# A two-layer decoder trunk on one core: ScalarE's reads of VectorE results issued a step later, the gated output in five stages, and eight weight residuals moved from GpSimd to VectorE

## The chip, the core and the metric

The kernel runs on one core of a Trainium2 chip. TensorE multiplies, VectorE, ScalarE and GpSimd work on the elements, and SyncE's queue issues the loads and stores. Each engine takes its instructions strictly in the order in which the program wrote them for that engine, and waits on semaphores for the others. The metric is the device time of one execution in microseconds (us). For the kernel before, three runs gave 849.0, 849.64 and 850.5 us.

## What is computed

Two layers over one sequence of 256 tokens of width 2048, in float32. Layer 0 runs retention heads and latent attention heads side by side and is not touched by the change. Layer 1, the Conformer convolution module, is:

```
h = rms_norm(x, norm_g)
a, b, gate = jnp.split(h @ w_in, 3, axis=-1)
u = a * jax.nn.sigmoid(b)
u = lax.conv_general_dilated(
    u, conv_w[:, None, :].astype(u.dtype), window_strides=(1,),
    padding=[(CONV_KERNEL - 1, 0)], dimension_numbers=('NWC', 'WIO', 'NWC'),
    feature_group_count=CONV_WIDTH) + conv_b
u = jax.nn.silu(layer_norm(u, ln_g, ln_b))
return x + (u * jax.nn.silu(gate)) @ w_out
```

The convolution is depthwise, causal and 31 taps long. The layer norm needs the mean and the variance over all 2048 channels, so that nothing behind it can start before the last channel has been convolved.

## The kernel before

All activations lie transposed: 128 channels on the partitions, 256 tokens along the row. The 2048 channels are 16 blocks of 128.

**Three products for one.** Each float32 weight tile `raw` is split in two parts that TensorE can multiply at full rate: ScalarE rounds it (`whi`, L167), and the residual `raw - whi` is taken by VectorE or GpSimd (`wlo`, L88 by way of `tt`). The activations are split the same way. `mm3` (L193 to L195) then issues three matmuls: high by high, high by low, low by high.

**The stream.** `Stream` hands out the weights in units of 1 MB, each in two halves. The table at its start says for each unit whether VectorE (`V`) or GpSimd (`G`) takes the residual. `half(u, h)` is called by TensorE's loop before it uses a half: it issues the residual three halves ahead (`lo_to(j + 3)`) and the rounding four halves ahead (`hi_to(j + 4)`), and then calls `tick()`. There are three buffers for `raw`, five for `whi` and four for `wlo`.

**The clock of the program.** `clock` counts halves: a half is 24 matmuls. `later(n, fn)` writes `fn` into the program n steps from now; `tick()` writes what is due, `tick(True)` does so in the middle of a half. Nothing of this runs on the chip: it decides the order in which instructions stand in each engine's queue.

**The order of layer 1.** `pair` multiplies 256 output columns (two blocks of 128) over all 2048 inputs, in four halves. Sixteen pairs give a and b of one channel block each; `glu` takes each pair: `norm_cols` multiplies it in PSUM by the token norm `R1` (VectorE), ScalarE takes the sigmoid, VectorE multiplies (`f`), and `conv_add` queues the 31 taps of this block. Two blocks are convolved in turn, a tap is one `stt` on VectorE. `pace` writes up to 2.88 us of such taps into the program at each step, by fixed costs for each operation; `spend` books other work of VectorE against the same budget. The residuals of the weights are not booked. `shift` and `centre` subtract an estimate of the mean, `centre_sq` squares on ScalarE, `centre_add` sums up both. Behind the sixteen pairs, eight pairs give the gate (`cgt`), with `norm_cols` and a SiLU each.

**The end of the layer norm.** When the last block is summed, `norm_conv` puts the sums through two matmuls (L985, L986), works out mean and scale, and then the result z in eight parts of 512 columns: `za` subtracts, scales (VectorE) and takes the SiLU (ScalarE), `zb` multiplies by the gate (VectorE) and rounds (ScalarE), `zc` takes the residual (VectorE). A list `z_todo` holds these steps; `z_tick` writes two of them at each step. The first product of the output, `kgroup` over `u_co1` with eight PSUM columns, eats one block k (half a part of z) per half; `z_need` sees to it that the part stands in the program before its use. Four more pairs (`u_co2`) and the stores end the kernel.

Of the kernel before, what the change touches and what calls it, by code (L numbers as in the profile page):

```python
# [10 lines left out]
AF = mybir.ActivationFunctionType  # L11
ALU = mybir.AluOpType
# [4 lines left out]
T = 256  # L17
# [8 lines left out]
TAPS = 31  # L26
# [22 lines left out]
def body(ctx, tc, a):  # L49
    nc = tc.nc  # L50
    act = nc.scalar.activation
    V = nc.vector
    G = nc.gpsimd
# [27 lines left out]
    def auxps():  # L81
        return psx.tile([P, 512], F32, tag="aux", name=nm("aux"))
# [4 lines left out]
    def tt(out, in0, in1, op, eng=None):  # L87
        (eng or V).tensor_tensor(out=out, in0=in0, in1=in1, op=op)  # L88

    def stt(out, in0, s, in1, op0, op1):  # L90
        V.scalar_tensor_tensor(out=out, in0=in0, scalar=s, in1=in1, op0=op0, op1=op1)  # L91
# [10 lines left out]
    def later(n, fn):  # L102
        due.append((clock[0] + n, len(due), fn))
# [84 lines left out]
    st = Stream()  # L188

    def mm3(ps, l, r, start, stop):  # L190
        (lh, ll), (rh, rl) = l, r
        mm = nc.tensor.matmul
        mm(ps, lh, rh, start=start, stop=False, skip_group_check=True)  # L193
        mm(ps, lh, rl, start=False, stop=False, skip_group_check=True)  # L194
        mm(ps, ll, rh, start=False, stop=stop, skip_group_check=True)  # L195
# [26 lines left out]
    u_gate = [st.add(a["w_in"][20 + i], V) for i in range(16)]  # L222
    u_out = [st.add(a["w_out"][i], V) for i in range(16)]
    u_ab = [st.add(a["c_in"][i], V if i < 2 else G) for i in range(32)]
    u_cg = [st.add(a["c_in"][32 + i], G) for i in range(16)]
    u_co1 = [st.add(a["c_out1"][i], V) for i in range(8)]
    u_co2 = [st.add(a["c_out2"][i], V) for i in range(8)]

# [95 lines left out]
    def kgroup(units, ncols, nk, rhs, hook=None, bank=mmps):  # L324
        banks = [bank() for _ in range(ncols // 2)]
        total = len(units) * nk
        k = 0
        for u in units:
            for h in range(2):
                if hook:  # L330
                    hook(k)
                hi, lo = st.half(u, h)
                for i in range(nk // 2):
                    r = rhs(k)
                    cols = []
                    for c in range(ncols):
                        o = (i * ncols + c) * P
                        ps = banks[c // 2][:, (c % 2) * T:(c % 2 + 1) * T]
                        if k > 0:
                            mm3(ps, (hi[:, o:o + P], lo[:, o:o + P]), r, False, k == total - 1)  # L340
                            continue
                        for n in range(2):
                            nc.tensor.matmul(ps, hi[:, o:o + P], r[n], start=c % 2 == 0 and n == 0, stop=False, skip_group_check=True)
                        cols.append((ps, lo[:, o:o + P]))
                    for ps, wl in cols:
                        nc.tensor.matmul(ps, wl, r[0], start=False, stop=False, skip_group_check=True)
                    k += 1
        return banks

    def pair(us, rhs):  # L350
        ps = mmps()
        for k in range(KT):
            if k % 4 == 0:
                hi, lo = st.half(us[k // 8], k // 4 % 2)
            elif k % 4 == 2:
                tick(True)
            for c in range(2):
                w = slice((k % 4 * 2 + c) * P, (k % 4 * 2 + c + 1) * P)
                mm3(ps[:, c * T:(c + 1) * T], (hi[:, w], lo[:, w]), rhs(k), k == 0 and c == 0, k == KT - 1)
        return ps  # L360
# [430 lines left out]
    for j in range(8):  # L791
        o = (j % 4) * 512
        ps = pair(u_gate[2 * j:2 * j + 2], xrhs)
# [23 lines left out]
    for j in range(8):  # L817
        ps = pair(u_out[2 * j:2 * j + 2], mrhs)
        o = (j % 4) * 512
# [28 lines left out]
    def upad(c, lo, n):  # L848
        o = (c % 7) * UP + lo
        return upt[c // 7][:, o:o + n]  # L850
# [7 lines left out]
    def spend(us):  # L858
        budget[0] -= us
# [65 lines left out]
    def ds(c):  # L925
        return kk(dd, c)
# [48 lines left out]
    done4 = [False]  # L975

    zh, zl = [], []
    z_todo = []
    ln_done = [False]
    held = []  # L980
    gates = [0]

    def norm_conv():
        lps = auxps()
        nc.tensor.matmul(lps[:, 0:T], ones[:, :], sums[:, 0:T], start=True, stop=True)  # L985
        nc.tensor.matmul(lps[:, T:512], ones[:, :], sums[:, T:512], start=True, stop=True)  # L986
        mu = tmp()
        V.tensor_scalar(out=mu[:, 0:T], in0=lps[:, 0:T], scalar1=1.0 / D, scalar2=None, op0=ALU.mult)
        tt(mu[:, T:512], mu[:, 0:T], mu[:, 0:T], ALU.mult)
        stt(mu[:, T:512], mu[:, T:512], -float(D), lps[:, T:512], ALU.mult, ALU.add)  # L990
        ls = e1[:, 0:T]
        rs_chain(ls, mu[:, T:512], D)
        nc.scalar.preload_act_table_set("silu_and_others")
        zh.extend([slot(12, F32R), slot(7, F32R)])
        zl.extend([slot(9, F32R), slot(10, F32R)])

        def pr(j):
            return dd[j // 4][:, (j % 4) * 512:(j % 4 + 1) * 512]

        def za(j):  # L1000
            d = pr(j)
            tt(two(d), two(d), both(mu[:, 0:T]), ALU.subtract)
            tt(two(d), two(d), both(ls), ALU.mult)
            for k in (2 * j, 2 * j + 1):
                act(ds(k), ds(k), AF.Silu, bias=cb[:, CB["lb"] + k:CB["lb"] + k + 1],
                    scale=cb[:, CB["lg"] + k:CB["lg"] + k + 1])

        def zb(j):
            d = pr(j)
            o = (j % 4) * 512  # L1010
            tt(d, d, cgt[j // 4][:, o:o + 512], ALU.mult)
            act(zh[j // 4][:, o:o + 512], d, AF.Copy)

        def zc(j):
            o = (j % 4) * 512
            tt(zl[j // 4][:, o:o + 512], pr(j), zh[j // 4][:, o:o + 512].bitcast(F32), ALU.subtract)

        for j in range(9):
            if j < 8:
                z_todo.append((0, lambda j=j: za(j)))  # L1020
            if j > 0:
                z_todo.append((j, lambda j=j: zb(j - 1)))
                z_todo.append((0, lambda j=j: zc(j - 1)))
        ln_done[0] = True
        for f in held[0]:
            f()
        z_tick()

    def z_step():
        if z_todo and z_todo[0][0] <= gates[0]:  # L1030
            z_todo.pop(0)[1]()
            return True
        return False

    def z_tick():
        for _ in range(2):
            z_step()
        if z_todo:
            later(1, z_tick)

    def z_need(k):
        while len(z_todo) > max(0, 24 - (1 + 3 * (k // 2 + 1))) and z_step():
            pass

    def conv_fin(c):
        ps = accs[c]
# [13 lines left out]
    def norm_cols(ps):  # L1060
        tt(two(ps[:, :]), two(ps[:, :]), both(R1[:, :]), ALU.mult)
        spend(0.6)

    def glu(c, ps):
        sg = tmp()
        norm_cols(ps)
        act(sg[:, 0:T], ps[:, T:512], AF.Sigmoid)  # L1067

        def f():
            tt(upad(c, TAPS - 1, T), ps[:, 0:T], sg[:, 0:T], ALU.mult)  # L1070
            conv_add(c)

        later(1, f)

    def conv_add(c):
        accs[c] = auxps()
        split[0] = c in (0, 15)
        lanes[c % 2].extend(conv_ops(c))
        spend(0.36)
# [5 lines left out]
    cgt = [slot(6), slot(1)]  # L1085
    for j in range(8):
        ps = pair(u_cg[2 * j:2 * j + 2], yrhs)
        o = (j % 4) * 512
        norm_cols(ps)

        def gate(j=j, ps=ps, o=o):
            act(cgt[j // 4][:, o:o + 512], ps[:, :], AF.Silu)
            gates[0] = j + 1
            z_step()
# [120 lines left out]
```

## Time and profile before

The profiled execution took 847.63 us by the same clock as the runs; its span from the first to the last instruction is 845.9 us.

| what | value |
|---|---|
| median of three runs | 849.64 us (849.0 to 850.5) |
| the profiled execution | 847.63 us |
| its span | 845.9 us |
| TensorE busy in the span | 98% |
| VectorE, ScalarE, GpSimd busy | 75%, 49%, 27% |
| mean granted TensorE clock | 0.996 |
| layer 1's first `norm_cols` on VectorE | 466.93 us |
| start of the two matmuls of the layer norm's sums, L985 | 718.75 us |
| start of the output product (first matmul of L343 into `aux`) | 744.75 us |

Times in views of the trace are in us from the start of the span. In a row of the timeline stand the start, the length, the engine, the line and the operation, what it writes and reads by the program's names, shapes, and in brackets how long the engine had been idle and which instruction let it go. `mm` and `aux` are PSUM tiles, `raw`, `whi`, `wlo` weight tiles, `s` the large SBUF slots, `t`, `e`, `m` and `R` smaller SBUF tiles, `cb` the constants. Line 88 is `tt`, line 91 `stt`, so that one line stands for many places of the kernel and the tiles tell them apart.

### The profile page before, as it was taken

How to read it: one execution, taken by the hardware profiler on the slowest of the kernel's cores; microseconds unless marked ns; L12 is line 12 of the kernel's file. 1: busy time of each engine (PE TensorE's matmuls, PEld its weight loads, DVE VectorE, ACT ScalarE, POOL GpSimd, SP SyncE). 2: the span in 40 equal slices, each digit the busy share in tenths (PEclk: the TensorE clock that was granted, in tenths of full speed). 3: DMA queues.
4: the chain of work that ended last, by engine and by line, in shares of the span. 5: the costliest groups of instructions: out<-in, count | busy, mean ns of one | idle time of the engine just before them, and what ended most of it. 6: DMA issues, size and time to landing. Idle time of an engine off the chain costs nothing.

```text
span 845.9 us, 16080 instructions
## 1 busy us (share of the span) xinstructions
PE 827.8 (98%) x6592; PEld 814.1 (96%) x6592; DVE 633.3 (75%) x1143; ACT 417.8 (49%) x593; POOL 225.6 (27%) x123
## 2 busy tenths in 40 slices
PE   8999999999999999999999999998999999879998
PEld 8999999999999999999999999998999999779998
DVE  6887555798686745765556699999999999787542
ACT  6766444556456445754446444424444454565331
POOL 0000000000000000000002788848788888400000
PEclk9999999999999999999999999999999999999999
DMA  8865454445445435545554545544455564246650
GB/s 286 326 238 191 163 199 154 147 150 194 155 150 199 150 107 189 201 167 184 199 200 138 211 154 197 201 142 143 164 199 201 178 202 170 100 122 243 234 174 26
DMA packets 24121, 151.16 MB, mean 179 GB/s; under 512 B 2800, under 2 KB 3952, under 8 KB 6896
## 3 DMA queue, kind: packets, MB, share of 16 engines
q1 hardware_dynamic: 23616, 148.03, 50.7%
q0 software_dynamic: 288, 2.10, 0.6%
q8 instruction: 51, 0.84, 0.4%
q14 instruction: 22, 0.18, 0.1%
q10 hardware_dynamic: 144, 0.03, 0.0%
HBM read 148.04 MB, written 2.10 MB: 177 GB/s over the span
## 4 chain that ended last, share of the span: by engine, by line
PE 83%; DVE 11%; ACT 2%; DMA 2%; issue 1%; SPq 0%; POOL 0%; DVEq 0%; ACTq 0%; POOLq 0%
PE mm L195 25%; PE mm L194 25%; PE mm L193 25%; DVE aux L91 4%; DVE s L88 3%; PE aux L195 2%; PE aux L193 1%; PE aux L194 1%; DVE wlo L88 1%; ACT whi L167 1%; DVE mm L88 1%; DMA raw<-in_w_first 1%; DMA raw<-in_w_in 1%; DVE t L88 1%; PE aux L639 0%
## 5 line engine op out<-in xcount | busy, mean ns | idle before, releaser
L195 PE MATMUL mm<-s,wlo 128*128 128x256 f32 x1788 | 508.3, 284 | 7.8 <-POOL wlo L88 6.7
L193 PE MATMUL mm<-s,whi 128*128 128x256 f32 x1788 | 511.2, 286 | 1.3 <-ACT whi L167 1.3
L194 PE MATMUL mm<-s,whi 128*128 128x256 f32 x1788 | 507.0, 284 | 0.0
L167 ACT ACTIVATE whi<-raw 128x1024 fp32r<-128x1024 f32 (+2 forms) x278 | 280.4, 1031 | 154.5 <-PE mm L194 93.1
L195 PEld LDWEIGHTS mm<-s,wlo 128*128 128x128 f32 x1788 | 344.2, 192 | 9.8 <-POOL wlo L88 7.7
L193 PEld LDWEIGHTS mm<-s,whi 128*128 128x128 f32 x1788 | 344.1, 192 | 2.6 <-ACT whi L167 1.9
L194 PEld LDWEIGHTS mm<-s,whi 128*128 128x128 f32 x1788 | 344.2, 192 | 0.7
L88 DVE TENSOR_TENSOR wlo<-raw,whi 128x1024 fp32r<-128x1024 f32 (+2 forms) x186 | 219.5, 1193 | 91.5 <-PE mm L195 52.1
L88 POOL TENSOR_TENSOR wlo<-raw,whi 128x1024 fp32r<-128x1024 f32 x92 | 220.0, 2422 | 65.0 <-ACT whi L167 49.1
L91 DVE SCALAR_TENSOR_TENSOR aux<-s,cb,aux 128x256 f32<-128x256 f32 x478 | 198.7, 482 | 8.3 <-ACT aux L870 3.4
L689 POOL MEMSET s<- 64x256 f32 x8 | 2.9, 362 | 232.4 <-PE mm L195 162.7
L193 PE MATMUL mm<-whi,s 128*128 128x272 f32 (+1 forms) x184 | 59.3, 322 | 0.0
L194 PE MATMUL mm<-wlo,s 128*128 128x272 f32 (+1 forms) x184 | 58.9, 320 | 0.0
L195 PE MATMUL mm<-whi,s 128*128 128x272 f32 (+1 forms) x184 | 58.8, 319 | 0.0
L1067 ACT ACTIVATE t<-mm 128x256 f32<-128x256 f32 x16 | 6.2, 385 | 100.7 <-DVE mm L88 100.7
L195 PE MATMUL aux<-s,wlo 128*128 128x256 f32 x120 | 34.3, 286 | 3.7 <-DVE wlo L88 3.7
L195 PEld LDWEIGHTS mm<-whi,s 128*128 128x128 f32 x184 | 34.6, 188 | 2.3
L193 PEld LDWEIGHTS mm<-whi,s 128*128 128x128 f32 x184 | 34.7, 189 | 1.8
L194 PEld LDWEIGHTS mm<-wlo,s 128*128 128x128 f32 x184 | 34.6, 188 | 1.8
L193 PE MATMUL aux<-s,whi 128*128 128x256 f32 x120 | 34.0, 283 | 0.0
L194 PE MATMUL aux<-s,whi 128*128 128x256 f32 x120 | 33.9, 283 | 0.0
L853 POOL MEMSET s<- 128x30 f32 x16 | 1.1, 120 | 119.4 <-PE mm L195 103.6
(186 smaller groups left out, 579.3 us busy)
## 6 DMA issues: line engine op xcount, KB each, us to landing
raw<-in_c_in SPq DMA_DIRECT2D x48, 1024.0 KB, 4.9
raw<-in_w_in SPq DMA_DIRECT2D x36, 1024.0 KB, 4.9
raw<-in_w_out SPq DMA_DIRECT2D x16, 1024.0 KB, 5.0
raw<-in_c_out SPq DMA_DIRECT2D x16, 1024.0 KB, 4.9
raw<-in_w_rv SPq DMA_DIRECT2D x8, 1088.0 KB, 5.1
raw<-in_w_kvb SPq DMA_DIRECT2D x4, 1024.0 KB, 4.7
raw<-in_w_first SPq DMA_DIRECT2D x7, 512.0 KB, 4.8
raw<-in_w_qb SPq DMA_DIRECT2D x3, 1024.0 KB, 4.9
```

The source lines that it names most:

```text
L88: (eng or V).tensor_tensor(out=out, in0=in0, in1=in1, op=op)
L91: V.scalar_tensor_tensor(out=out, in0=in0, scalar=s, in1=in1, op0=op0, op1=op1)
L167: act(hi[:, :], self.raw[u][:, h * n:(h + 1) * n], AF.Copy)
L193: mm(ps, lh, rh, start=start, stop=False, skip_group_check=True)
L194: mm(ps, lh, rl, start=False, stop=False, skip_group_check=True)
L195: mm(ps, ll, rh, start=False, stop=stop, skip_group_check=True)
L689: G.memset(krz(i)[64 * b:64 * b + 64, :], 0.0)
L853: G.memset(upad(c, 0, TAPS - 1), 0.0)
L1067: act(sg[:, 0:T], ps[:, T:512], AF.Sigmoid)
```

## The change

It has four parts.

1. In `glu` the sigmoid is written one step behind the `norm_cols` that it reads, the product `f` two steps behind it (before: one), and `conv_add` three (before: one). In the gate pairs the SiLU is written one step behind its `norm_cols`.
2. z is written in five stages instead of three (`za`, `zs`, `zb`, `zr`, `zc`: the two ScalarE operations are now stages of their own), half a step apart, and its eight parts start two steps apart.
3. `kgroup` calls `tick(True)` in the middle of each half when its banks are `aux` ones, so that half steps exist in the output product too.
4. The residuals of the last four gate units (eight halves) are taken by VectorE instead of GpSimd.

```
-    u_cg = [st.add(a["c_in"][32 + i], G) for i in range(16)]
+    u_cg = [st.add(a["c_in"][32 + i], G if i < 12 else V) for i in range(16)]
...
                     for c in range(ncols):
+                        if bank is auxps and c == ncols // 2:
+                            tick(True)
...
+        def zs(j):
             for k in (2 * j, 2 * j + 1):
                 act(ds(k), ds(k), AF.Silu, bias=cb[:, CB["lb"] + k:CB["lb"] + k + 1],
                     scale=cb[:, CB["lg"] + k:CB["lg"] + k + 1])
...
+        def zr(j):
+            o = (j % 4) * 512
+            act(zh[j // 4][:, o:o + 512], pr(j), AF.Copy)
...
-        for j in range(9):
-            if j < 8:
-                z_todo.append((0, lambda j=j: za(j)))
-            if j > 0:
-                z_todo.append((j, lambda j=j: zb(j - 1)))
-                z_todo.append((0, lambda j=j: zc(j - 1)))
+        z_stage.extend([za, zs, zb, zr, zc])
...
+        for j in range(8):
+            later(2 * j, lambda j=j: z_run(j, 0))
+    def z_run(j, s):
+        if z_at[j] != s:
+            return
+        if s == 2 and gates[0] <= j:
+            later(0.5, lambda: z_run(j, s))
+            return
+        z_stage[s](j)
+        z_at[j] += 1
+        if z_at[j] < 5:
+            later(0.5, lambda: z_run(j, s + 1))
...
     def glu(c, ps):
-        sg = tmp()
         norm_cols(ps)
-        act(sg[:, 0:T], ps[:, T:512], AF.Sigmoid)
+        sg = []
+
+        def s():
+            sg.append(tmp())
+            act(sg[0][:, 0:T], ps[:, T:512], AF.Sigmoid)
 
         def f():
-            tt(upad(c, TAPS - 1, T), ps[:, 0:T], sg[:, 0:T], ALU.mult)
-            conv_add(c)
-
-        later(1, f)
+            tt(upad(c, TAPS - 1, T), ps[:, 0:T], sg[0][:, 0:T], ALU.mult)
+
+        later(1, s)
+        later(2, f)
+        later(3, lambda: conv_add(c))
...
-        if held and not ln_done[0]:
-            held[0].append(gate)
-        else:
-            gate()
+        def gate_when(gate=gate):
+            if held and not ln_done[0]:
+                held[0].append(gate)
+            else:
+                gate()
+
+        later(1, gate_when)
```

**ScalarE's queue at the first pair of layer 1.** `whi` rows are roundings, L1067 is the sigmoid, L868 and L870 are first taps of a channel block that ScalarE takes. Before:

```order
L167 ACTIVATE whi_5213<-raw_5022 128x1024
L1067 ACTIVATE t_5239<-mm_5109 128x256
L167 ACTIVATE whi_5247<-raw_5112 128x1024
L167 ACTIVATE whi_5277<-raw_5112 128x1024
L868 ACTIVATE aux_5262<-s_649_5087,cb 128x256
L870 ACTIVATE aux_5262<-s_649_5087,cb 128x256
```

And now (the sigmoid is L1076, the first taps L870 and L872):

```order
L167 ACTIVATE whi_5213<-raw_5022 128x1024
L167 ACTIVATE whi_5245<-raw_5112 128x1024
L1076 ACTIVATE t_5259<-mm_5109 128x256
L167 ACTIVATE whi_5275<-raw_5112 128x1024
L167 ACTIVATE whi_5306<-raw_5183 128x1024
L167 ACTIVATE whi_5335<-raw_5183 128x1024
L870 ACTIVATE aux_5320<-s_649_5087,cb 128x256
L872 ACTIVATE aux_5320<-s_649_5087,cb 128x256
```

One rounding now stands ahead of the sigmoid instead of behind it, and two more roundings stand ahead of the first taps: the convolution begins two steps later in the program. On TensorE's queue the two matmuls of the sums move by the same two steps, from row 5502 to row 5550, 48 matmuls nearer to the output product, whose first matmul is row 5660 in both.

**VectorE's queue at the end of the convolution**, from the last two blocks' sums to the mean. `mm_5108` holds the running sums, the two rows into `e_4086` are the last sums, the `mm<-mm,R` row is a `norm_cols`, the row that reads `aux` without `cb` after that is the mean. Before:

```order
L88 TENSOR_TENSOR mm_5108<-mm_5108,t_8242 128x256
L91 SCALAR_TENSOR_TENSOR aux_7513<-s_651_5089,cb,aux_7513 128x256 x7
L88 TENSOR_TENSOR t_8315<-t_8315,e_4086 128x256
L88 TENSOR_TENSOR s_653_5107<-aux_7513,t_8315 128x256
L88 TENSOR_TENSOR e_4086<-mm_5108,s_653_5107 128x256
L88 TENSOR_TENSOR e_4086<-mm_5108,t_8349 128x256
L88 TENSOR_TENSOR mm_8229<-mm_8229,R_4087 128x512
L988 TENSOR_SCALAR t_8429<-aux_8426 128x256
```

And now:

```order
L88 TENSOR_TENSOR mm_5108<-mm_5108,t_8300 128x256
L88 TENSOR_TENSOR mm_8213<-mm_8213,R_4087 128x512
L88 TENSOR_TENSOR wlo_8364<-raw_8140,whi_8328 128x1024
L91 SCALAR_TENSOR_TENSOR aux_7571<-s_651_5089,cb,aux_7571 128x256 x4
L88 TENSOR_TENSOR wlo_8399<-raw_8216,whi_8368 128x1024
L91 SCALAR_TENSOR_TENSOR aux_7571<-s_651_5089,cb,aux_7571 128x256 x3
L88 TENSOR_TENSOR t_8404<-t_8404,e_4086 128x256
L88 TENSOR_TENSOR s_653_5107<-aux_7571,t_8404 128x256
L88 TENSOR_TENSOR e_4086<-mm_5108,s_653_5107 128x256
L88 TENSOR_TENSOR e_4086<-mm_5108,t_8410 128x256
L88 TENSOR_TENSOR wlo_8439<-raw_8216,whi_8401 128x1024
L88 TENSOR_TENSOR wlo_8469<-raw_8288,whi_8443 128x1024
```

Of the eight residuals that GpSimd gives up, five stand ahead of the last sums (three of them further up), two between the sums and the mean, and one behind the first part of z. The `norm_cols` that stood behind the sums stands ahead of them.

**ScalarE's queue at the first parts of z.** L1005 and L1008 are the SiLU of z, L1012 and L1017 its rounding, L1092 and L1102 the SiLU of a gate pair. Before:

```order
L1092 ACTIVATE s_878_7487<-mm_8229 128x512
L1005 ACTIVATE s_652_5106<-s_652_5106,cb 128x256 x4
L1012 ACTIVATE s_964_8443<-s_652_5106 128x512
L167 ACTIVATE whi_8474<-raw_8306 128x1024
L1005 ACTIVATE s_652_5106<-s_652_5106,cb 128x256 x2
L167 ACTIVATE whi_8507<-raw_8306 128x1024
L1012 ACTIVATE s_964_8443<-s_652_5106 128x512
```

And now:

```order
L167 ACTIVATE whi_8526<-raw_8366 128x1024
L1008 ACTIVATE s_652_5106<-s_652_5106,cb 128x256 x2
L1102 ACTIVATE s_877_7471<-mm_8363 128x512
L167 ACTIVATE whi_8558<-raw_8366 128x1024
L1017 ACTIVATE s_969_8502<-s_652_5106 128x512
L167 ACTIVATE whi_8592<-raw_8441 128x1024
L1008 ACTIVATE s_652_5106<-s_652_5106,cb 128x256 x2
```

A rounding of weights now stands between any two ScalarE operations of z that wait for VectorE, and the tiles that are rounded there are already those of the output product (`raw_8366` on), where before the last gate units (`raw_8306`) were still to be rounded.

More of the change, by code (lines that the diff above doesn't have):

```diff
@@ L977, in body @@
     zh, zl = [], []
-    z_todo = []
     ln_done = [False]
@@ L1008, in zb @@
         def zb(j):
-            d = pr(j)
             o = (j % 4) * 512
-            tt(d, d, cgt[j // 4][:, o:o + 512], ALU.mult)
-            act(zh[j // 4][:, o:o + 512], d, AF.Copy)
+            tt(pr(j), pr(j), cgt[j // 4][:, o:o + 512], ALU.mult)
+        def zr(j):
+            o = (j % 4) * 512
+            act(zh[j // 4][:, o:o + 512], pr(j), AF.Copy)
         def zc(j):
@@ L1026, in norm_conv @@
             f()
[L1027 to L1039, printed above, removed]
-    def z_need(k):
-        while len(z_todo) > max(0, 24 - (1 + 3 * (k // 2 + 1))) and z_step():
-            pass
+        for j in range(8):
+            later(2 * j, lambda j=j: z_run(j, 0))
+    z_stage = []
+    z_at = [0] * 8
+    def z_run(j, s):
[8 more added lines that the diff above has]
+            later(0.5, lambda: z_run(j, s + 1))
+    def z_need(k):
+        j = k // 2
+        while z_at[j] < 5:
+            assert z_at[j] < 2 or gates[0] > j
+            z_stage[z_at[j]](j)
+            z_at[j] += 1
     def conv_fin(c):
@@ L1093, in gate @@
             gates[0] = j + 1
-            z_step()
-        if held and not ln_done[0]:
-            held[0].append(gate)
-        else:
-            gate()
+        def gate_when(gate=gate):
[4 more added lines that the diff above has]
+        later(1, gate_when)
     while not ln_done[0]:
```

## The prediction

> **What bounds the kernel now.** I read the page's busy times first, then the busy time by stage, then who waited for whom in the convolution.
>
> ```profile
> PE 827.8 (98%) x6592; PEld 814.1 (96%) x6592; DVE 633.3 (75%) x1143; ACT 417.8 (49%) x593; POOL 225.6 (27%) x123
> ...
> 467.00:718.00 251.00, 248.07 (x2050) 247.21 (x2049) 240.15 (x569) 107.69 (x146) 202.82 (x86) 0.99 0.53 179
> 718.00:744.70 26.70, 22.44 (x167) 21.46 (x165) 19.64 (x22) 14.23 (x22) 10.43 (x5) 0.94 0.34 118
> 744.70:760.00 15.30, 11.29 (x86) 10.52 (x87) 12.78 (x17) 9.80 (x16) 0.00 (x0) 1.00 0.30 78
> 760.00:842.00 82.00, 82.00 (x685) 81.88 (x683) 42.33 (x43) 30.14 (x32) 0.00 (x0) 1.00 0.50 175
> ```
>
> In the rows by stage stand the stretch, its length, the busy time of TensorE, its weight loads, VectorE, ScalarE and GpSimd, then the granted clock. TensorE is the bound: full from 760 on, and short by 2.9 us in the convolution (467 to 718), 4.3 around the layer norm and 4.0 as the output product begins. Some 11 us, and what a lowered clock adds, are all that another order can win there. But in the convolution VectorE is busy 240 of 251 us, and ScalarE waits for it:
>
> ```profile
> ACT t L1067 <- DVE mm L88: 100.7, 16, 10.5
> POOL wlo L88 <- ACT whi L167: 44.9, 19, 7.2
> ...
> PE mm L195 <- POOL wlo L88: 2.6, 3, 2.0
> ...
> L88 DVE TENSOR_TENSOR mm<-mm,R 128x512 f32<-128x512 f32 x22 | 15.2, 691 | 1.8 <-PE mm L195 1.8
> ```
>
> VectorE works behind the program there, the sigmoid (L1067) holds ScalarE for up to 10.5 us, the roundings behind it come late, GpSimd's residuals too, and now and then TensorE waits. The last row is `norm_cols` in that stretch: its 22 calls found VectorE idle for TensorE once, 1.8 us, which is the first call. So VectorE is never ahead, and **the convolution's end is set by VectorE, not by TensorE.** TensorE's waits in that stage are then no gain by themselves. What counts is when the last sums are ready, and how long it takes from there to the output product.
>
> ```profile
> 717.38 0.42 DVE L88 TENSOR_TENSOR e<-mm,t 128x256 f32<-128x256 f32 x1
> 717.72 0.69 DVE L88 TENSOR_TENSOR mm<-mm,R 128x512 f32<-128x512 f32 x1
> ...
> 718.75 0.43 PE aux L985 x2
> 719.18 0.45 PE aux L986 x2
> ...
> 744.75 0.39 PE L343 MATMUL aux<-s,whi 128*128 128x256 f32 x1 [0.27 <-ACT whi L167]
> ...
> 841.85 0.12 PE mm L194
> 841.97 0.13 PE mm L195
> ```
>
> Sums ready at 717.80 (717.38 + 0.42), output product from 744.75, last matmul done at 842.1. One matmul takes 0.12 us.
>
> **The change, part by part.**
>
> *Sigmoid and gate SiLU a step later.* One rounding that stood behind each waiting sigmoid now stands ahead of it, so TensorE has one half more patience with VectorE (24 matmuls, 2.9 us). No operation is added. I book this at nothing in the convolution, for the reason above: TensorE only comes sooner to a place where it waits for the sums.
>
> *`conv_add` two steps later.* The taps start two halves later, 48 x 0.12 = 5.76 us.
>
> ```profile
> 471.88 8.36 DVE L91 SCALAR_TENSOR_TENSOR aux<-s,cb,aux 128x256 f32<-128x256 f32 x16 [3.37 <-ACT aux L870]
> ```
>
> VectorE is idle for 3.37 us ahead of its first tap now; then it will be idle 5.76 longer, and a stream that is never ahead does not get that back. The two matmuls of the sums move by the same 48 matmuls, so TensorE's work up to the output product stays the same.
>
> *Eight residuals by VectorE.* Five stand ahead of the last sums, and one `norm_cols` moves ahead of them too.
>
> ```profile
> 745.86 1.22 DVE L88 TENSOR_TENSOR wlo<-raw,whi 128x1024 fp32r<-128x1024 f32 x1
> ...
> 749.01 1.14 DVE wlo L88
> ```
>
> 5 x 1.22 = 6.1 us, and 0.6 for the `norm_cols` (0.69, less the overlap of neighbours). Nothing covers them, as VectorE is the late engine; behind each stand the taps, and behind those the sums.
>
> *Additions that GpSimd holds up.* In `shift` and `centre` seven additions of two SBUF tiles take 4.48 + 2.51 + 3.68 = 10.7 us. An addition of that size takes 0.42 (the sums above), so 7.7 us are lost, and GpSimd is at work all the while:
>
> ```profile
> 541.18 4.48 DVE L88 TENSOR_TENSOR t<-s 128x256 f32<-128x256 f32 x2
> 545.69 2.51 DVE L88 TENSOR_TENSOR t<-t 128x256 f32<-128x256 f32 x1
> 564.78 3.68 DVE L88 TENSOR_TENSOR s<-s,e 128x256 f32<-128x256 f32 x4
> ...
> 540.42 10.05 POOL L88 TENSOR_TENSOR wlo<-raw,whi 128x1024 fp32r<-128x1024 f32 x4 [1.07 <-ACT whi L167]
> ```
>
> It ran four residuals without a gap, since ScalarE had been held and then gave it four roundings at once. With roundings that come evenly there are gaps. This term is open: with all seven free it is -7.7; with all seven held, 2.5 each, 17.5 - 10.7 = +6.8. I take -1.8, about one held addition less, near the row, because GpSimd stays almost as busy as it is (203 of 251 us).
>
> Sums ready: 717.80 + 5.76 + 6.1 + 0.6 - 1.8 = **728.5**. TensorE could be at L985 between 719.5 (718.75 + 5.76, less all that it now loses in the convolution, about 5 with the clock) and 724.5. So the change puts a new wait of 4 to 9 us there, first for residuals of the last gate units, then for the sums. Behind it on TensorE's queue stand 108 matmuls of the gate and then the output product; ScalarE's next roundings wait for the buffers that those free, but they are four halves ahead. A load is issued once the residual of three units earlier is done, four halves (11.5 us) ahead of its rounding, and lands in 4.9 us:
>
> ```profile
> raw<-in_c_in SPq DMA_DIRECT2D x48, 1024.0 KB, 4.9
> ```
>
> I cost it at nothing; if VectorE is later than 6.6 us with a residual, the rounding slips by the excess.
>
> *From the sums to the output product.* TensorE needs 0.1 + 0.43 + 0.45 for the sums' matmuls and 108 x 0.12 = 12.96 for the rest: 14.0 us. Against this stands the chain to the first part of z:
>
> ```profile
> 719.65 0.42 DVE L988 TENSOR_SCALAR t<-aux 128x256 f32<-128x256 f32 x1 [1.24 <-PE aux L986]
> 720.11 2.42 DVE L88 TENSOR_TENSOR t<-t 128x256 f32<-128x256 f32 x1
> ...
> 723.02 1.92 DVE L85 TENSOR_SCALAR t<-t 128x256 f32<-128x256 f32 x1
> ...
> 726.79 0.42 DVE L91 SCALAR_TENSOR_TENSOR e<-t,t 128x256 f32<-128x256 f32 x1
> ...
> 732.88 2.72 DVE L88 TENSOR_TENSOR s<-s,e 128x512 f32<-128x512 f32 x1
> ...
> 738.23 2.47 DVE L88 TENSOR_TENSOR s<-s,s 128x512 fp32r<-128x512 f32 x1 [2.03 <-ACT s L1012]
> ...
> 747.00 0.68 DVE L88 TENSOR_TENSOR s<-s,t 128x512 f32<-128x512 f32 x1
> ...
> 732.61 2.44 POOL L88 TENSOR_TENSOR wlo<-raw,whi 128x1024 fp32r<-128x1024 f32 x1 [7.82 <-PE mm L195]
> 737.81 2.34 POOL L88 TENSOR_TENSOR wlo<-raw,whi 128x1024 fp32r<-128x1024 f32 x1 [2.76 <-issue]
> ```
>
> Mean to scale took 7.56 us (719.65 to 727.21), with 2.42 and 1.92 for two operations that need about 0.43 each when nothing holds them: 4.1. In z the rows of 2.72 and 2.47 start while GpSimd runs a residual; the same size takes 0.68 without it. GpSimd will be done by then. So, from the sums: two residuals 2.75 (the second waits for a rounding), mean to scale 4.1, the two operations of `za` 1.3, `norm_cols` 0.6, then residual, `zb`, residual, next `za`, `zc`: 1.13 + 0.65 + 1.13 + 1.3 + 0.65. That is 13.6 us, 0.4 less than TensorE's way. From there VectorE needs 2 x 1.13 + 1.3 + 0.65 + 0.65 = 4.9 us for each part of z, 5.5 with a `norm_cols`, and TensorE takes 5.76: z stays ahead.
>
> *The clock.*
>
> ```profile
> 740.00:745.00 5.00, 4.52 (x24) 4.23 (x25) 3.20 (x5) 2.93 (x5) 0.15 (x1) 0.66 0.62 210
> 755.00:760.00 5.00, 2.88 (x24) 2.68 (x24) 4.00 (x6) 3.20 (x5) 0.00 (x0) 1.00 0.20 29
> ...
> 740.21 0.39 PE L195 MATMUL mm<-s,wlo 128*128 128x256 f32 x1 [1.97 <-POOL wlo L88]
> ...
> 758.55 0.39 PE L195 MATMUL aux<-s,wlo 128*128 128x256 f32 x1 [2.12 <-DVE wlo L88]
> ...
> PE aux L195 <- DVE wlo L88: 3.7, 2, 2.1
> PE aux L346 <- DVE wlo L88: 0.2, 1, 0.2
> ```
>
> After the wait that ended at 740.21 the clock fell, which cost (1 - 0.66) x 5 = 1.7 us; after the one that ended at 758.55 it did not. The longer wait ahead of L985 may cost 0 to 1.7, and I take 1.2. The Trainium skill (TensorE: Matmul & The Clock Gate, Part 1: The HAM clock gate) has the clock fall after a whole idle window of some 3.4 us on a free-running grid. By that rule a wait of 1.97 us costs nothing, which the first of these rows contradicts; a wait of 5.3 us would hold a whole window in about 55 of 100 cases, and this term would be 0.9, as an estimate.
>
> Output product from 728.5 + 14.0 + 1.2 = 743.7 instead of 744.75: 1.1 us won. Behind it TensorE's waits of 3.7 and 0.2 us (the last two rows) go, as z stays ahead and no residual stands behind a waiting part of z: 3.9 us. The rest is as before. Middle ticks and stages add no instruction. **Sum: -5.0 us**, from the profiled execution's 847.63 (span 845.9, and 1.7 around it) to 842.6. The median of the runs shown lies 2.0 above that execution, so the forecast is 849.64 - 5.0 = **844.6 us**.
>
> **The rivals.**
>
> *More is won.* GpSimd holds up few additions and the clock stays: sums at 725, product at 739.0, so 5.8 + 3.9 = 9.7 us less, 839.9. For it: whether an addition is held hangs on where GpSimd happens to be. Against: GpSimd is busy four fifths of that stage.
>
> *The wait only moves.* If one or two more additions are held than now (2.1 each), the sums come at 732.4 or 734.5, the product at 747.6 or 749.7, 2.9 or 5.0 late, which eats the 3.9 us behind it: 848.6 to 850.7. The change then does what its words say, and nothing comes of it.
>
> *Slower: a residual costs VectorE what it costs GpSimd.* If GpSimd, late itself, still runs when VectorE takes its first five residuals, each is held like the rows at 732.88 and 738.23: 2.5 us for 1.2, five times, 6.4 more. Sums at 734.9, product at 750.1, 5.4 late, less 3.9: +1.5, and with a second dip of the clock +3.2: 851.1 to 852.8. It decides from sums at 744.75 + 3.9 - 15.2 = 733.5 on. Against: GpSimd gets no new work behind the twelfth gate unit, and one of its residuals lasts 2.4 us, so that it should hold one, not five.
>
> **How the numbers follow.** The forecast, with the clock's ends and one held addition either way 841.3 to 847.2, gets 0.61; more won 0.14; the wait only moves 0.16; slower 0.09. A measurement of this kernel can tell about 0.2%, 1.7 us, from no change. So faster 0.75, same 0.16, slower 0.09. The range for 8 in 10 runs from 840.0 to 849.5.
>
> **What would show it.** L985 (now L986) starts near 728.6, behind an idle TensorE; waits for `wlo` on VectorE stand in the halves ahead of it. The row at 720.11 shrinks to 0.43. The product starts near 743.7, no wait of TensorE stands behind it, and ScalarE's 100.7 us of waiting for VectorE shrink. I am wrong if the sums come before 725 or after 732 (then the taps did not move as a block, or the held additions are not as I took them), if the product starts over 15.7 us behind the sums (then z sets its start), or if TensorE waits again behind it.

## The result, and the profile after

The changed kernel takes 838.97 us (four runs, 838.1 to 839.63) against 849.36 us for the kernel before in the same comparison (849.0 to 850.5): a ratio of 0.9875, with a 95% interval of 0.9858 to 0.9892. That is 10.4 us less, twice the 5.0 that were forecast, and below the predicted range of 840.0 to 849.5. The profiled execution took 839.34 us, its span 837.6. One execution of the kernel before in a later comparison took 3874.92 us and is left out of the ratios and spreads below.

The busy times of the page, then busy time by stage with the limits moved to the same events (first pair to the sums' matmuls, to the output product, its first 15 us, the rest), and all of TensorE's waits from the first pair of layer 1 on:

```profile
PE 826.2 (99%) x6592; PEld 814.5 (97%) x6592; DVE 632.5 (76%) x1151; ACT 422.0 (50%) x593; POOL 207.5 (25%) x115
...
467.00:725.00 258.00, 252.80 (x2104) 252.33 (x2102) 243.85 (x573) 113.37 (x148) 195.39 (x82) 1.00 0.52 179
725.00:741.40 16.40, 16.31 (x112) 15.95 (x113) 14.39 (x23) 12.93 (x18) 0.00 (x0) 0.83 0.38 129
741.40:757.00 15.60, 15.60 (x132) 15.60 (x132) 15.39 (x20) 11.38 (x17) 0.00 (x0) 1.00 0.62 209
757.00:834.00 77.00, 76.79 (x640) 76.58 (x639) 40.93 (x45) 28.36 (x33) 0.00 (x0) 1.00 0.46 160
...
PE aux L986 <- DVE e L88: 4.3, 1, 4.3
PE mm L195 <- POOL wlo L88: 1.0, 1, 1.0
```

TensorE now waits at two places instead of ten: 1.0 us in the convolution, and 4.3 us for the sums (the code has moved down a line or more, so L985 of before is L986 now, and the sigmoid L1076). In the output product it waits for nothing. What it still loses stands almost all at the sums: the wait ahead of them, and the clock of 0.83 behind it. The timeline there, of VectorE and then of TensorE:

```profile
704.70 1.22 DVE L88 TENSOR_TENSOR wlo<-raw,whi 128x1024 fp32r<-128x1024 f32 x1
...
720.71 1.22 DVE L88 TENSOR_TENSOR wlo<-raw,whi 128x1024 fp32r<-128x1024 f32 x1
...
725.06 0.42 DVE L88 TENSOR_TENSOR e<-mm,t 128x256 f32<-128x256 f32 x1
...
729.02 0.42 DVE L88 TENSOR_TENSOR t<-t 128x256 f32<-128x256 f32 x1
...
720.56 0.28 PE L195 MATMUL mm<-s,wlo 128*128 128x256 f32 x1
725.09 1.22 PE L986 MATMUL aux<-e,ones 128*128 128x256 f32 x2 [4.25 <-DVE e L88]
...
741.47 0.64 PE L345 MATMUL aux<-s,whi 128*128 128x256 f32 x4
...
833.51 0.28 PE L195 MATMUL mm<-s,wlo 128*128 128x256 f32 x1
```

Five residuals between 704.70 and 720.71 (two of them shown) stand ahead of the sums, each 1.21 to 1.22 us. TensorE started its last matmul ahead of them at 720.56 and began the sums' matmuls at 725.09. The sums were complete at 725.48, not at 728.5 as forecast; the product began at 741.47, not 743.7; from there to the last matmul are 92.0 us (before 97.1).

Where ScalarE and VectorE waited for each other in the convolution (first ScalarE's row of after; then VectorE's waits for the first taps that ScalarE takes, before and after):

```profile
ACT t L1076 <- DVE mm L88: 54.9, 15, 8.3
...
DVE aux L91 <- ACT aux L870: 3.4, 1, 3.4
DVE aux L91 <- ACT aux L868: 2.1, 4, 1.0
...
DVE aux L91 <- ACT aux L872: 9.0, 1, 9.0
```

ScalarE's wait at the sigmoid fell from 100.7 us to 54.9. VectorE's one wait ahead of the very first tap grew as forecast (3.4 to 9.0), but its four other waits for a first tap, 2.1 us, are gone; the prediction had not counted them. From the first tap to the sums VectorE took 247.6 us (before 245.9), though five residuals, 5.7 us from start to start, were new in it.

### The profile page after: what moved, and what is told of

The parts are those of the page before. It is cut to its first block, busy times and chain, and to the rows that moved or that the text cites. A ratio compares the mean times of both kernels' runs of the same rounds, so it can differ in the third digit from the quotient of the medians.

```text
span 837.6 us, 16060 instructions
## 1 busy us (share of the span) xinstructions
PE 826.2 (99%) x6592; PEld 814.5 (97%) x6592; DVE 632.5 (76%) x1151; ACT 422.0 (50%) x593; POOL 207.5 (25%) x115
## 4 chain that ended last, share of the span: by engine, by line
PE 76%; DVE 20%; issue 1%; ACT 1%; DMA 1%; POOL 1%; SPq 0%; DVEq 0%; POOLq 0%; ACTq 0%
PE mm L195 22%; PE mm L193 22%; PE mm L194 22%; DVE aux L91 13%; DVE mm L88 2%; DVE s L88 2%; PE aux L195 2%; PE aux L194 2%; PE aux L193 2%; DVE wlo L88 1%; DVE t L88 1%; DMA raw<-in_w_first 1%; POOL wlo L88 1%; ACT whi L167 0%; PE aux L641 0%
## 5 line engine op out<-in xcount | busy, mean ns | idle before, releaser
L88 DVE TENSOR_TENSOR wlo<-raw,whi 128x1024 fp32r<-128x1024 f32 (+2 forms) x194 | 229.4, 1193 | 87.3 <-PE mm L195 52.3
L88 POOL TENSOR_TENSOR wlo<-raw,whi 128x1024 fp32r<-128x1024 f32 x84 | 201.9, 2415 | 44.5 <-ACT whi L167 21.9
L1076 ACT ACTIVATE t<-mm 128x256 f32<-128x256 f32 x16 | 6.1, 384 | 54.9 <-DVE mm L88 54.9
```

Source lines behind the costliest of these rows:

```text
L1076: act(sg[0][:, 0:T], ps[:, T:512], AF.Sigmoid)
```

## Experiments

One sum is used for all kernels. In a stream that never waits, matmuls start 0.12 us apart. **Lost** is the sum, over all neighbouring matmuls from the first `norm_cols` of layer 1 on, of what the distance of their starts has over 0.12 (differences of a few ns, which even out, are not counted); waits and a lowered clock both count. It is split at the sums' matmuls, so that a wait ahead of these counts to the middle part, and at the output product, and worked out from each kernel's one trace to some 0.1 us. (The sums' matmuls themselves are 0.3 to 0.5 of the middle part in every kernel.) The times of the sums and of the product are counted from the first `norm_cols` of layer 1, which lay between 466.66 and 469.18 us. Median and ratio are of the timed runs; the median of before was 848.5 to 848.7 in these comparisons, 849.36 in that of the changed kernel.

| kernel | median, us | ratio to before, 95% interval | sums ready | product starts | lost: to the sums / to the product / behind |
|---|---|---|---|---|---|
| before | 848.5 | | 250.9 | 277.8 | 5.5 / 7.1 / 5.0 |
| changed | 838.97 | 0.9858 to 0.9892 | 258.3 | 274.3 | 1.6 / 7.4 / 0.0 |
| late_only | 839.46 | 0.9876 to 0.9918 | 253.6 | 267.4 | 1.6 / 0.5 / 6.1 |
| z_only | 840.80 | 0.9891 to 0.9929 | 250.9 | 271.2 | 5.5 / 0.5 / 4.4 |
| res_only | 845.46 | 0.9949 to 0.9971 | 253.8 | 276.3 | 5.5 / 5.6 / 3.2 |
| late_z | 834.73 | 0.9810 to 0.9853 | 253.6 | 267.3 | 1.6 / 0.5 / 0.6 |
| glu_only | 839.05 | 0.9874 to 0.9910 | 252.9 | 268.1 | 1.6 / 1.3 / 5.1 |
| gate_only | 846.03 | 0.9964 to 0.9983 | 250.9 | 276.1 | 5.5 / 5.3 / 4.9 |
| taps_only | 844.76 | 0.9938 to 0.9969 | 258.1 | 274.1 | 8.4 / 0.5 / 4.5 |
| sig_taps1 | 840.58 | 0.9886 to 0.9927 | 249.1 | 269.0 | 0.3 / 3.5 / 6.6 |
| late_res | 843.73 | 0.9926 to 0.9963 | 258.4 | 273.5 | 1.6 / 6.6 / 4.1 |
| res14 | 833.60 | 0.9803 to 0.9846 | 253.8 | 267.4 | 1.6 / 0.5 / 0.3 |
| after_lag | 840.54 | 0.9892 to 0.9933 | 258.4 | 271.1 | 1.6 / 4.2 / 3.7 |
| late_z_t2 | 831.10 | 0.9780 to 0.9814 | 247.1 | 266.0 | 0.3 / 0.5 / 0.0 |

The table holds together: 848.5 less the difference of the lost sums (before 17.6) gives each of the other thirteen medians within 1.2 us. So, to that measure, TensorE's lost time is the whole of every difference, and the rest is to find what makes TensorE lose it.

### The parts alone: late_only, z_only, res_only, and all but the residuals: late_z

late_only is before with the hunks of `glu` and `gate_when`; z_only is before with the five stages and the middle ticks; res_only has one line; late_z is the changed kernel with that line undone:

```
res_only, on before:
-    u_cg = [st.add(a["c_in"][32 + i], G) for i in range(16)]
+    u_cg = [st.add(a["c_in"][32 + i], G if i < 12 else V) for i in range(16)]
late_z, on the changed kernel: the same line back to G
```

> Only the sigmoid, f, conv_add and gate SiLU later; z in three stages and all residuals as before. Theory A (VectorE sets the convolution's end; what ScalarE no longer holds back gives VectorE its first taps on time): VectorE's 2.2 us of waiting for L868 in the convolution go, the sums come at 719 to 721 (717.8 + 5.76 for the later taps, less about 3 for the first taps and 1 to 2 for held additions), TensorE does not wait for them, but z now has 48 matmuls (5.76 us) less to hide behind, so that the waits around the layer norm grow: time 846 to 851. Theory B (TensorE's waits in the convolution were the loss): those 5 us go and nothing comes in their place, 844 to 845.

> Only z in five stages half a step apart, with the middle ticks; sigmoids and residuals as before. Theory A: sums as before at 717.8, TensorE's waits behind the start of the output product (4 to 5 us) go, but GpSimd still runs the last residuals and holds VectorE's operations of z, so the product starts between 741 and 745: time 841 to 846. Theory B (the later sigmoids carry the gain): 847 or more.

> Only the last eight gate residuals by VectorE. Theory A: three of them ahead of the sums add 3.6 us, sums at 721.4; mean to scale takes 4.1 instead of 7.6 us, and z is not held by GpSimd (4 us), but two residuals stand between sums and mean and roundings still stand behind waiting parts of z: time 845 to 850. Theory B: VectorE loses 8 x 1.2 us where it is late, 852 or more.

> The change without its residuals: GpSimd keeps the last eight. Theory A: sums at about 719.5 (725.5 less 5 x 1.2), before TensorE reaches L986 (720.6), so no wait there and no fall of the clock; but mean to scale takes 7.6 us again and the first parts of z are held by GpSimd; product between 739 and 744, no waits behind it or few: time 836 to 842. Theory B (the residuals carry the gain behind the layer norm): 844 or more.

The delays alone gave 9.1 us, and both theories missed it. The sums came 2.7 us later than before, as theory A had it, but the waits around the layer norm, which it expected to grow, all but went: what TensorE lost up to the product fell from 12.6 to 2.1 us, and behind the product it rose from 5.0 to 6.1. z_only gave 7.7, just beyond theory A's range, and not in its way: most of the loss behind the product stayed (4.4 of 5.0), and the loss between the sums and the product went (7.1 to 0.5), where theory A had GpSimd still hold VectorE. res_only gave 3.1, as theory A had it. The three do not add: late_z, without the residuals, is **faster** than the changed kernel, by 4.2 us (3.7 by their ratios to before), and faster than either of its theories had it. With the delays in, the residuals cost. Behind the product it is the delays and the stages together that count: alone they leave 6.1 and 4.4 us of loss there, together 0.6. Why it takes both was not tested.

### What of the delays counts: glu_only, gate_only, taps_only, sig_taps1

All on before. glu_only takes the new `glu`, gate_only the new `gate_when`. taps_only leaves the sigmoid and `f` where they were and moves only the taps; sig_taps1 moves the sigmoid and puts the taps one step later instead of two:

```
taps_only, on before:
             tt(upad(c, TAPS - 1, T), ps[:, 0:T], sg[:, 0:T], ALU.mult)
-            conv_add(c)
         later(1, f)
+        later(3, lambda: conv_add(c))
sig_taps1, on glu_only:
-        later(3, lambda: conv_add(c))
+        later(2, lambda: conv_add(c))
```

> The kernel before with the sigmoid, the product f and conv_add written later, and the gate's SiLU as before. Theory A (the sigmoid is what counts: ScalarE no longer stands waiting in the convolution, so VectorE's taps and TensorE both lose their waits there): sums near 720.4 as with both delays together, TensorE's 2.9 us of waits in the convolution down to about 1.2, the clock's dip there gone; the waits between the sums and the output product (4.3 us and a dip) stay, so the product starts near 740 and the whole is 843 to 846. Theory B (the place of the gate's SiLU decides nothing, and all of the 9 us of the two delays comes from here): product near 734.5, 838 to 841.

> The kernel before with only the gate's SiLU written a step later. Theory A (it frees ScalarE's roundings of the last gate units, so that TensorE's waits of 4.3 us between the sums and the output product go, and nothing in the convolution): sums at 717.8 as before, product at 738 to 740, then waits of some 3 to 5 us behind it, whole 843 to 846. Theory B (no effect): sums, product and whole as before, 848 to 850.

> The kernel before with conv_add alone two steps later; the sigmoid and f as before. Theory A (the later taps only move the sums and the work around them; VectorE gets none of the 5.76 us back while ScalarE still stands waiting at the sigmoid): sums near 723.5, product within 2 us of before's 744.75, whole 847 to 851. Theory B (the later place of the taps is itself the gain, since the first taps of ScalarE and the sums' matmuls then stand further behind): sums at 720 to 721, product 736 to 740, whole 840 to 845.

> The kernel before with the sigmoid one step later, f one step later and conv_add one step later instead of two; the gate's SiLU as before. Theory A (the sigmoid's place decides): the same as with conv_add two steps later, within 1.5 us, the sums some 0 to 3 us earlier. Theory B (the place of the taps decides): half of that kernel's gain.

glu_only is as fast as both delays together, so theory B of that run held: the gate's SiLU adds nothing to it, though alone it gave 2.7 us. taps_only and glu_only, whose taps are equally late, differ only in the place of the sigmoid and of the `f` that needs it, and there lie 5.7 us of time, 5.2 us in the sums and 6.8 us of TensorE's loss in the convolution. ScalarE's timeline around the longest wait, in taps_only and then in glu_only, with TensorE's stop in taps_only between them:

```profile
575.08 1.04 ACT L167 ACTIVATE whi<-raw 128x1024 fp32r<-128x1024 f32 x1
576.03 0.55 ACT L868 ACTIVATE aux<-s,cb 128x256 f32<-128x256 f32 x1
585.84 0.38 ACT L1067 ACTIVATE t<-mm 128x256 f32<-128x256 f32 x1 [9.27 <-DVE mm L88]
586.12 1.99 ACT L167 ACTIVATE whi<-raw 128x1024 fp32r<-128x1024 f32 x2
...
587.23 0.58 PE L193 MATMUL mm<-s,whi 128*128 128x256 f32 x1 [4.21 <-ACT whi L167]
...
572.73 0.55 ACT L868 ACTIVATE aux<-s,cb 128x256 f32<-128x256 f32 x1
573.23 1.04 ACT L167 ACTIVATE whi<-raw 128x1024 fp32r<-128x1024 f32 x1
582.55 0.39 ACT L1070 ACTIVATE t<-mm 128x256 f32<-128x256 f32 x1 [8.28 <-DVE mm L88]
```

In taps_only the sigmoid stands right behind a first tap, and the rounding that TensorE needs next stands behind the sigmoid: 9.27 us of ScalarE's waiting become 4.21 of TensorE's. In glu_only one rounding more stands ahead of the sigmoid; ScalarE still waits 8.28 us, and TensorE 1.0. In taps_only the sums were ready at 725.55 and TensorE came to their matmuls only at 727.76: there TensorE's stops, not VectorE, set the end of the convolution. VectorE even waited for TensorE's products and for the sigmoid, which in glu_only it did not behind its first tap:

```profile
DVE mm L88 <- PE mm L195: 1.2, 4, 0.5
...
DVE s L88 <- ACT t L1067: 0.4, 1, 0.4
```

Theory B of taps_only half held too. Its sums came 7.3 us later than before, worse than the 5.76 of the moved taps, as theory A had it. But its time fell by 3.9 us, into theory B's range, because what TensorE lost between sums and product went from 7.1 to 0.5. A likely reason is in ScalarE's queue there, in before:

```profile
724.98 0.42 ACT L207 ACTIVATE t<-t 128x256 f32<-128x256 f32 x1 [4.31 <-DVE t L85]
...
731.43 1.04 ACT L167 ACTIVATE whi<-raw 128x1024 fp32r<-128x1024 f32 x1
735.64 1.09 ACT L1005 ACTIVATE s<-s,cb 128x256 f32<-128x256 f32 x2 [3.16 <-DVE s L88]
736.64 1.04 ACT L167 ACTIVATE whi<-raw 128x1024 fp32r<-128x1024 f32 x1
```

The roundings of the last gate units stand behind ScalarE's waits for the mean and for z. Written two steps later, the layer norm stands behind more of these roundings. z in stages cures the same place in another way (z_only 0.5), so that this part of the two gains cannot be had twice. sig_taps1 shows the trade the other way: earlier taps, 0.3 lost in the convolution, but 3.5 and 6.6 at the end; its time is 1.5 us above glu_only's, at the edge of what theory A allowed. gate_only came out between its two theories and left 5.3 of the 7.1: the gate's SiLU is not the main thing that holds the roundings there.

### Where the residuals cost: late_res, res14, after_lag, and the best version: late_z_t2

late_res is the changed kernel with z as before. The others are single lines:

```
res14, on the changed kernel:
-    u_cg = [st.add(a["c_in"][32 + i], G if i < 12 else V) for i in range(16)]
+    u_cg = [st.add(a["c_in"][32 + i], G if i < 14 else V) for i in range(16)]
after_lag, on the changed kernel:
-LN_LAG = 2.5
+LN_LAG = 3.5
late_z_t2, on late_z:
-        later(3, lambda: conv_add(c))
+        later(2, lambda: conv_add(c))
```

> The changed kernel with z as before (the list and two steps of it at each step), so both delays and the eight residuals. Theory A (the five residuals ahead of the last sums cost VectorE 6.1 us and TensorE comes to the sums' matmuls just in time without them, so all of it is new waiting): sums near 725, a wait of 4 to 5 us ahead of the sums' matmuls, product near 740, part of TensorE's 6 us of waits and gaps behind the product gone: whole 841 to 844, above the two delays alone. Theory B (the residuals repay themselves at the end, as without the delays, where they gave 3 us): 836 to 838.

> The changed kernel with only the last two gate units (four halves) given to VectorE instead of four (eight). Theory A (only residuals ahead of the last sums cost; one is left ahead of them instead of five): sums 4 to 5 us earlier than in the changed kernel, TensorE waits under 1.5 us for them, whole 834 to 836. Theory B (the cost of the residuals lies behind the sums, where VectorE also works out the mean and z): 837 to 839.

> The changed kernel with the sums' two matmuls written one half later (2.88 us of TensorE's work more ahead of them, as much less behind). Theory A (TensorE's idle time ahead of the sums is the whole loss, and the chain from the sums to the first part of z is shorter than TensorE's rest): idle time there down to 1 to 2 us, product 1 to 3 us earlier, whole 836 to 838. Theory B (with less of TensorE's work behind the sums, the chain to z sets the product's start): product at sums + 13.6 to 16, a wait just ahead of it, whole 838 to 841.

> The changed kernel without the residuals, and conv_add one step earlier. Theory A (all that can be won is TensorE's waiting, of which 2 to 3 us are left without the residuals, 1.3 of them in the convolution, where they fell to 0.2 with the earlier taps): 833 to 835, TensorE's waits from the first pair on under 2 us. Theory B (the earlier sums put more of the gate's work behind them and ScalarE's roundings wait again): 836 to 838.

late_res against late_only and the changed kernel against late_z are the same edit on two grounds, and it cost 4.3 and 4.2 us of time, and 4.8 and 4.7 us in the sums. In late_only TensorE came to the sums' matmuls just as they were ready (sums 720.44, matmuls from 720.37), so all that VectorE does more ahead of them is waiting of TensorE. res14 leaves one residual ahead of the sums instead of five, and the whole cost is gone: 833.6, sums as in late_z. Theory A held in both; res14 was 0.4 us faster than its range.

after_lag missed with theory A: the wait for the sums fell (4.3 to 1.4 us), but the time did not. Theory B's wait and time came, with the product 12.7 us behind the sums. TensorE's timeline where the output product begins:

```profile
736.49 0.28 PE L195 MATMUL mm<-s,wlo 128*128 128x256 f32 x1
738.69 0.38 PE L345 MATMUL aux<-s,whi 128*128 128x256 f32 x1 [1.92 <-ACT s L1017]
741.01 0.80 PE L345 MATMUL aux<-s,whi 128*128 128x256 f32 x2 [1.95 <-DVE s L88]
```

With less of TensorE's own work behind the sums the product's first two blocks wait for z: L1017 is the rounding of its first part, and VectorE's `s` the residual of that part (`zc`). So moving the two matmuls by one half won nothing; other places were not tried.

late_z_t2 is the fastest of all, 831.1 us, 1.9 us below the range of its theory A. Busy time by stage, from the first pair on:

```profile
466.60:716.00 249.40, 249.40 (x2079) 249.35 (x2078) 235.78 (x569) 114.28 (x149) 207.59 (x88) 1.00 0.53 184
716.00:732.70 16.70, 16.70 (x138) 16.59 (x137) 13.29 (x17) 10.58 (x16) 6.98 (x3) 1.00 0.38 128
732.70:825.00 92.30, 92.30 (x770) 92.12 (x768) 56.87 (x64) 40.93 (x49) 0.00 (x0) 1.00 0.49 169
```

TensorE is busy all the time at the full clock, and the sums are ready 2.3 us ahead of their matmuls (713.73 and 716.00). By the sum of the table 0.8 us are left in this layer for another order of the same matmuls. The earlier taps, which alone brought waits back at the end (sig_taps1), bring none with z in stages.

## Why the prediction was wrong

The sign was right, the size was half. Against the profiled executions: the sums came 3.0 us earlier than forecast, the way from there to the product was 0.8 longer (16.0 instead of 15.2), and behind the product 5.0 instead of 3.9 were won, 1.1 more. That is 3.3 us (842.6 forecast, 839.34 measured). The other 2.4 are the step to the median: 2.0 were added, and the changed kernel's median lies 0.4 below its profiled run.

- **The step that failed: "Sigmoid and gate SiLU a step later ... I book this at nothing in the convolution".** The place of the sigmoid, with `f`, is worth 5.7 us where the residuals stay with GpSimd (glu_only against taps_only). The reason given was that VectorE is never ahead, so that TensorE's waits there are no gain. The first half of it was read from `norm_cols` alone. VectorE did wait, in its taps, for first taps that ScalarE held behind the sigmoid (the row of 2.1 us above). The second half fails in taps_only, where TensorE's stops set the end. Of the 5.2 us between the sums of the two, additions held up by GpSimd account for 2.4 (11.6 against 9.2), VectorE's waits for TensorE's products and for the sigmoid for 1.7, the 478 taps with the waits ahead of them for 1.0. In the changed kernel TensorE does, as forecast, only come sooner to a place where it waits for the sums; what the step missed there is that the sums themselves come sooner. Of the 3.0 us, 2.2 are the time that VectorE no longer stands idle ahead of a tap. The changed kernel with the sigmoid in its old place was not run, so what the step is worth in it as a whole stays open.
- **"The convolution's end is set by VectorE, not by TensorE"** was a near tie, and the prediction's own rows had it the other way round: the sums were ready at 717.80, and TensorE came to their matmuls later, at 718.58 by its timeline and without a wait (718.75 in the prediction's chain). Both engines lost time while ScalarE stood at the sigmoid, and both got a part of it back in glu_only: TensorE lost 1.6 instead of 5.5 us up to the sums, and VectorE took 242.2 instead of 245.9 us from its first tap to them. Had those 2.1 us of VectorE's or TensorE's 2.9 us been taken as the lower end of that step, the range would have held the time.
- **"The taps start two halves later, 5.76 us ... a stream that is never ahead does not get that back"** was right as far as it went: the first tap came 5.75 us later against the first pair, and in taps_only nothing of it came back; in glu_only 3.7 us of it did. That the later place of the sums by itself frees the end (3.9 us gained in spite of it) was not seen as a part of this edit, but booked under the end as a whole.
- **Five residuals, 6.1 us, and a `norm_cols`, 0.6** were right in number, length and place; the residuals moved the sums by 4.7 to 4.8 us instead of 6.1. The rival in which GpSimd holds each of them did not occur.
- **Held additions, -1.8**: the seven took 1.33 + 2.52 + 5.37 = 9.2 instead of 10.7 us, -1.5. That the guess came so near was luck: in other kernels they took 6.2 (late_z_t2) to over 11 us (taps_only), so it could have gone 2 to 3 us either way.
- **Sums to product.** TensorE set the product's start, as forecast, and mean to scale took 3.9 us (forecast 4.1). The wait at the sums, forecast as 4 to 9 us, was 4.3. The clock cost more than the 1.2 taken: at 0.83 over 16.4 us it is 2.8.
- **Behind the product** no wait was left, as forecast. It was worth 5.0 instead of 3.9, because the waits' rows give only the idle time, from the end of one matmul to the start of the next. Each of the three longer stops cost 0.26 us more from start to start, and two short ones, 0.3 us together, are hardly in the rows; 97.1 less 92.0 counts it all.
- **The median.** The runs of before spread from 847.1 to 850.5 us over all comparisons, with a granted clock from 0.998 (847.1) to 0.994 (850.25, but also 847.42). Its profiled execution, 0.996 and 847.63, was one of the better ones; the changed kernel's, at 0.995, was one of the worse of four at 0.995 to 0.998. The difference of one profile to its median does not carry over to another kernel.

Of the rivals "more is won" came nearest in numbers (sums at 725, 839.9 us), but not for its reason: the clock did fall, and the held additions stayed near the forecast.

## What to carry to other kernels

When an engine in the middle stands waiting for a late engine, ask what is queued behind the waiting instruction: moving that instruction one step back, behind the next thing that others need, was worth 5.7 us here and left the late engine's own work as it was. Before a wait is booked at nothing because "the other engine is late anyway", look for the rows in which that other engine waits too, since both can be held by the same instruction. Work moved to another engine costs time where it stands ahead of something for which the bound engine waits: the same eight residuals won 3.1 us in one order and cost some 4 in the next, and moving only the last four of them cost nothing.

## What the runs showed of the hardware

**Taps on one block against two in turn.** In the changed kernel's timeline the first block's taps, in turn on the two halves of one PSUM tile, and later ones, alternating between two tiles:

```profile
482.02 6.78 DVE L91 SCALAR_TENSOR_TENSOR aux<-s,cb,aux 128x256 f32<-128x256 f32 x13
...
602.51 5.18 DVE L91 SCALAR_TENSOR_TENSOR aux<-s,cb,aux 128x256 f32<-128x256 f32 x13
```

The same thirteen operations took 0.52 us each on one tile and 0.40 on two. In every kernel here 64 or 65 of the 478 taps take 0.45 to 0.6 us from start to start, so this is not what moved the sums.

**GpSimd and VectorE.** In late_z_t2, VectorE's scaling by a constant in the layer norm and a multiplication of z, and the two GpSimd residuals beside them:

```profile
718.94 2.31 DVE L85 TENSOR_SCALAR t<-t 128x256 f32<-128x256 f32 x1
726.02 2.08 DVE L88 TENSOR_TENSOR s<-s,s 128x512 f32<-128x512 f32 x1 [1.16 <-ACT s L1008]
...
718.70 2.40 POOL L88 TENSOR_TENSOR wlo<-raw,whi 128x1024 fp32r<-128x1024 f32 x1 [0.53 <-PE mm L195]
725.14 2.41 POOL L88 TENSOR_TENSOR wlo<-raw,whi 128x1024 fp32r<-128x1024 f32 x1 [4.04 <-ACT whi L167]
```

GpSimd's end at 721.10 and 727.55, VectorE's at 721.25 and 728.10: VectorE's operation, 0.29 us in the changed kernel, where GpSimd is idle, finished 0.15 us behind the residual, and the multiplication, 0.68 us without it, 0.55 behind. The Trainium skill (SBUF — State Buffer, SBUF: two separate sides) has VectorE and GpSimd share one pair of ports by an exclusive lock for the whole of an instruction; these rows agree.

**The clock after a wait.** Windows of 3.4 us (TensorE's busy time, granted clock), first the changed kernel and then late_res, around the wait of 4.3 us for the sums that both have:

```profile
723.70:727.10 3.40, 2.01 (x5) 0.50 0.00 0
727.10:730.50 3.40, 3.40 (x18) 0.50 0.79 270
...
724.80:728.20 3.40, 2.19 (x7) 0.70 0.00 0
728.20:731.60 3.40, 3.40 (x25) 0.80 0.86 299
```

After the same wait the changed kernel had two such stretches at half the clock and late_res two at 0.70 and 0.80; by the sum of the experiments the way from there to the product then lost 2.9 and 2.1 us. late_only, with waits of up to 1.9 us, ran at a mean granted clock of 0.999, while before lost 1.7 us of its clock after a wait of 1.97. A single trace does not settle a term of 0 to 3 us of this kind.
